# Twelve of 22 pairs of up tiles as seven block products for eight, and the inner tiles of one feed-forward in three parts

## The chip, the cores and the metric

The kernel runs on one core of one Trainium2 chip. The metric is the time of one execution on the device, in microseconds (us). A core has these engines: TensorE (PE) multiplies matrices, and its weight loads are shown apart as PEld; VectorE (DVE) and ScalarE (ACT) work on elements; GpSimd (POOL) does a few small operations; SyncE (SP) issues the DMA transfers. Each has its own queue of instructions and works it off in order; semaphores tie them together. Matmul results go to eight banks of 128 x 512 float32 (names b_...).

## The reference: what is computed

The reference is a float32 network for 256 latent tokens and 256 context tokens of width 1024. A first block (gated linear attention and a squared-ReLU feed-forward) is followed by two layers whose norms and residual sums are modulated by a conditioning vector: layer 0 with neighbourhood attention over latents and context, layer 1 with grouped-query attention. The change is in the feed-forward of layer 0, which runs over latents (h) and context (hc) with the same weights:

```python
def swiglu_ffn(h, w_in, w_out):
    a, g = jnp.split(h @ w_in, 2, axis=-1)
    return (jax.nn.silu(a) * g) @ w_out

h  = h  + g2_l * swiglu_ffn(ada_norm(h,  norm_ffn[i], sh2_l, sc2_l), ffn_w_in[i], ffn_w_out[i])
hc = hc + g2_c * swiglu_ffn(ada_norm(hc, norm_ffn[i], sh2_c, sc2_c), ffn_w_in[i], ffn_w_out[i])
```

`w_in` is 1024 x 5632, `w_out` 2816 x 1024. The modulation vectors (shifts, scales, gates g2_l, g2_c and the same for layer 1) are products of the conditioning vectors with a 1024 x 6144 matrix for each layer.

## The kernel before

**Products.** Every float32 product is made of three matmuls in a reduced format: each operand x is split into h (x rounded, an ACT copy) and l = x - h (a DVE subtract), and `mm3` issues h*h, l*h and h*l (lines 193, 194, 195). So a block of 128 x 128 weights by n token columns costs three matmuls.

**Weights.** All weights pass as a list of units (`UNITS`), each a tile of 128 x 1024. `w_load` sends a unit by SP into one of five "raw" buffers (512 KB), `w_split` makes its h on ACT (L178) and its l on DVE (L179) in two of the "w" buffers, and `wnext` hands it to the matmuls and runs the loads and splits some units ahead.

**The feed-forward of layer 0.** The 2816 inner features are 22 tiles of 128. For each, a pair of units (one of `a`, one of the gate `g`, each 1024 x 128) is multiplied with the transposed, normalised tokens `fT` (all 512 columns): 2 x 8 x 3 = 48 matmuls of 512 columns (`ffn_up`). The first two pairs run in two halves of 256 columns (`ffn_up_first`), while the latents are still transposed. Behind a pair, `ffn_act` makes Silu on ACT (L1111), the product with the gate on DVE (L1112) and the split of the result (ACT L1118, DVE L1119). The 22 tiles go in two parts of 11. After each part `ffn_down0` multiplies them with the down units: one bank for each of the token tiles 0 to 3 (0, 1 latents; 2, 3 context), half of the 1024 output columns (`hf`) at a time, and `gated` multiplies the banks with the modulation's gate and adds them to the residual (DVE L1080, L1081). In part 0 all four token tiles run together. In part 1 the context tiles run first, both halves, so that their normalisation (`normed`, L219) can run while the latents run; within the latents' last half, after some inner tiles, the context's transposes for layer 1 are issued (`to_T`, PE L232, then DVE and ACT conversions L248 to L251).

**The modulation.** The rest of the modulation vectors is computed on DVE beside all this: `ada_run(adaC, n)` takes n steps; a step loads a 128 x 1024 tile of the conditioning matrix by SP into one of two "ada" buffers and reduces it against the conditioning vector (L324, a multiply with a sum along the row), for some of the steps twice, for latents and context (double steps). Before, each up pair takes two steps and each down unit one.

**Order.** The code names the work in the order in which it is written, but a tile scheduler orders the instructions on each engine by its own estimate. What runs when on an engine is therefore seen in the compiled order, of which some rows are shown with the change.

## Time and profile before

| | us |
|---|---|
| runs shown: median of 3 (lowest to highest) | 1257.70 (1257.22 to 1257.75) |
| profiled execution, its own time | 1256.72 |
| its span in the trace | 1254.9 |
| PE busy | 1244.0 |
| DVE busy | 919.9 |
| ACT busy | 688.2 |
| the changed stage in the trace (first up pair to the end of the down product) | about 562 to 944 |

The profiled execution is 1.0 us below the median of the runs. The stage's up pairs of part 0 run to about 694, the down product of part 0 to about 755, the up pairs of part 1 to about 866, and the rest is the down product of part 1. In the rows below, "x" is a count, a name in front of "<-" is what is written, and the name behind "<-" in a row of waits is what was waited for. A row of a timeline begins with its start in us from the start of the span and its duration.

### The profile page before, as it was taken

What the parts mean: (1) busy time and instruction counts of PE and PEld (TensorE: products, weight loads), DVE (VectorE), ACT (ScalarE), POOL (GpSimd) and SP (SyncE); (2) the same over time, 40 slices, a digit from 0 to 9 for tenths busy, and PEclk for the clock granted to TensorE, in tenths of its full rate; (3) what the DMA queues carried; (4) which work ended last, traced back from release to release, by engine and by line L of the source; (5) the groups of instructions that cost most, each with busy time, mean ns of one, the idle gap of its engine ahead of it and who ended that gap; (6) DMA issues with size and microseconds to landing.
All of it is one profiled execution on the core that took longest, in us unless ns stands there. A gap on an engine that the chain in (4) does not pass through costs nothing.

```text
span 1254.9 us, 18667 instructions
## 1 busy us (share of the span) xinstructions
PE 1244.0 (99%) x6872; PEld 1043.2 (83%) x6872; DVE 919.9 (73%) x1638; ACT 688.2 (55%) x1344; POOL 78.7 (6%) x137
## 2 busy tenths in 40 slices
PE   9999999999999999999999999999999999999997
PEld 8888889898888777789888888887888777999997
DVE  6959888697989887777877767633667988655555
ACT  8575655666549888655232222323456897544443
POOL 1010000030100000001000000000003220000000
PEclk9999999999999999999999999999999999999999
DMA  8647687787673333463656877633662324656650
GB/s 304 189 151 237 192 289 268 271 277 246 198 249 111 105 110 118 160 197 118 213 177 206 259 266 249 205 100 102 197 204 76 113 84 131 219 187 185 186 185 34
DMA packets 68507, 231.22 MB, mean 184 GB/s; under 512 B 8048, under 2 KB 8736, under 8 KB 68416
## 3 DMA queue, kind: packets, MB, share of 16 engines
q1 hardware_dynamic: 68128, 229.68, 57.0%
q8 instruction: 54, 0.88, 0.3%
q10 hardware_dynamic: 288, 0.35, 0.1%
q14 instruction: 37, 0.30, 0.1%
HBM read 228.93 MB, written 1.07 MB: 183 GB/s over the span
## 4 chain that ended last, share of the span: by engine, by line
PE 95%; ACT 2%; DVE 1%; issue 1%; DMA 0%; POOL 0%; SPq 0%; POOLq 0%; ACTq 0%
PE b L193 28%; PE b L194 28%; PE b L195 28%; PE b L1000 2%; PE b L1469 1%; PE b L981 1%; PE b L232 1%; PE b L1455 1%; PE b L562 1%; PE b L962 1%; PE b L963 1%; PE b L951 1%; PE b L1436 1%; DVE wl L179 0%; DMA t<-in_xt_dram 0%
## 5 line engine op out<-in xcount | busy, mean ns | idle before, releaser
L178 ACT CAST wh<-raw 128x1024 fp32r<-128x1024 f32 (+1 forms) x308 | 320.7, 1045 | 392.8 <-PE b L194 292.4
L179 DVE TENSOR_TENSOR wl<-raw,wh 128x1024 fp32r<-128x1024 f32 (+1 forms) x308 | 372.5, 1216 | 154.9 <-ACT wh L178 151.9
L193 PE MATMUL b<-t,wh 128*128 128x256 f32 (+1 forms) x1120 | 365.7, 327 | 0.0
L194 PE MATMUL b<-t,wl 128*128 128x256 f32 (+1 forms) x1120 | 365.6, 327 | 0.0
L195 PE MATMUL b<-t,wh 128*128 128x256 f32 (+1 forms) x1120 | 365.3, 327 | 0.0
L193 PE MATMUL b<-wh,t 128*128 128x512 f32 (+1 forms) x748 | 299.2, 402 | 1.2 <-ACT t L250 0.6
L194 PE MATMUL b<-wh,t 128*128 128x512 f32 (+1 forms) x748 | 294.8, 394 | 0.0
L195 PE MATMUL b<-wl,t 128*128 128x512 f32 (+1 forms) x748 | 294.7, 394 | 0.0
L193 PEld LDWEIGHTS b<-t,wh 128*128 128x128 f32 x1120 | 210.7, 188 | 22.2
L194 PEld LDWEIGHTS b<-t,wl 128*128 128x128 f32 x1120 | 210.8, 188 | 21.9
L195 PEld LDWEIGHTS b<-t,wh 128*128 128x128 f32 x1120 | 210.5, 188 | 20.4 <-DVE t L251 0.2
L195 PEld LDWEIGHTS b<-wl,t 128*128 128x128 f32 x748 | 140.4, 188 | 34.2
L193 PEld LDWEIGHTS b<-wh,t 128*128 128x128 f32 x748 | 140.4, 188 | 32.2 <-ACT t L250 1.0
L194 PEld LDWEIGHTS b<-wh,t 128*128 128x128 f32 x748 | 140.8, 188 | 30.1 <-DVE t L251 0.5
L324 DVE CUSTOM_DVE_ANT_0 a<-a,crow 128x1024 f32<-128x1024 f32 x96 | 117.6, 1233 | 28.8 <-DMA a<-in_ada_dram 28.3
L324 DVE CUSTOM_DVE_ANT_0 t<-a,crow 128x1024 bf16<-128x1024 f32 x64 | 78.5, 1237 | 7.3 <-DMA a<-in_ada_dram 7.1
L1112 DVE TENSOR_TENSOR t<-b,t 128x512 f32<-128x512 f32 (+1 forms) x42 | 23.7, 564 | 59.4 <-PE b L195 52.2
L205 POOL TENSOR_TENSOR c<-c,mhalf 128x1 f32<-128x1 f32 x21 | 14.2, 676 | 539.0 <-DVE c L204 538.9
L339 POOL TENSOR_TENSOR mod<-mod,bcol 128x8 f32<-128x8 f32 x20 | 13.4, 671 | 475.1 <-DVE mod L324 472.7
L1118 ACT CAST t<-t 128x512 fp32r<-128x512 f32 (+1 forms) x42 | 21.7, 516 | 28.6 <-DVE t L1112 28.6
L212 ACT ACTIVATE t<-t 128x512 f32<-128x512 f32 x40 | 24.8, 624 | 10.8 <-DVE t L1081 6.4
L1445 ACT ACTIVATE t<-b,c,c 128x512 f32<-128x512 f32 x32 | 26.0, 812 | 3.5 <-POOL c L1443 3.5
(244 smaller groups left out, 1212.6 us busy)
## 6 DMA issues: line engine op xcount, KB each, us to landing
raw<-in_wst_dram SPq DMA_DIRECT2D x310, 512.0 KB, 4.4
a<-in_ada_dram SPq DMA_DIRECT2D x96, 512.0 KB, 4.4
t<-in_rpb_dram SPq DMA_DIRECT2D x16, 256.0 KB, 4.5
t<-row SPq DMA_DIRECT2D x12, 256.0 KB, 5.1
t<-in_ctx_dram SPq DMA_DIRECT2D x8, 256.0 KB, 5.6
t<-in_xt_dram SPq DMA_DIRECT2D x4, 256.0 KB, 5.8
t<-in_x_dram SPq DMA_DIRECT2D x4, 256.0 KB, 6.5
crow<-in_cvec_dram SPq DMA_DIRECT2D x2, 512.0 KB
```

Source lines behind the costliest of these rows:

```text
L178: A.copy(out=h[:, :n], in_=raw[:, :n])
L179: V.tensor_tensor(out=l[:, :n], in0=raw[:, :n], in1=h[:, :n], op=ALU.subtract)
L193: T.matmul(o, lhsT=lh, rhs=rh, start=first, stop=False)
L194: T.matmul(o, lhsT=ll, rhs=rh, start=False, stop=False)
L195: T.matmul(o, lhsT=lh, rhs=rl, start=False, stop=last)
L205: G.tensor_tensor(out=ms[:, 3:4], in0=ms[:, 2:3], in1=mhalf[:, 0:1], op=ALU.pow)
L212: A.activation(out=junk[hf], in_=halves[hf], func=AF.Square, scale=1.0 / 32.0, accum_out=ms[:, hf:hf + 1])
L324: V.tensor_tensor_reduce(out=raw if ci == n_c - 1 else t2([D], BF16), in0=raw, in1=crow[ci], scale=1.0, scalar=0.0, op0=ALU.mult, op1=ALU.add,
L1000: T.matmul(po[e * 64:(e + 1) * 64, cols_], lhsT=v, rhs=probs[(head, "l" if lat_q else "c")][:, c, :], start=(c == 0), stop=(c == n_c - 1))
L1112: V.tensor_tensor(out=a, in0=pg_[:, :n], in1=a, op=ALU.mult)
L1118: A.copy(out=h, in_=a)
L1445: A.activation(out=pl, in_=sl, func=AF.Exp, scale=r, bias=mx[:, 1:2], accum_out=mx[:, 2:3])
```

## The change

The 22 inner tiles go in three parts, 0 to 7, 8 to 15, 16 to 21 (`PARTS`), with a down product after each; there are 28 down units of full size instead of 36 of which six are half units. The tokens stand in two sets of 256 columns, `fL` (latents) and `fC` (context), so the ordinary pairs make 96 matmuls of 256 columns instead of 48 of 512.

From pair 10 on (`F_SEVEN`), a pair is computed in Strassen's manner. The pair's weights are a 2 x 2 matrix of blocks (a or g, by upper or lower half of the 1024 inputs), the tokens one too (half of the inputs, by latents or context). The ordinary product takes eight block products, the scheme seven, each of 4 x 3 matmuls of 256 columns: 84 a pair (`ffn_up7`). For it, sums of the weight blocks are made and split for each pair (`pair_sums`: DVE L1202, L1203, L1206, L1209; three full splits, ACT L1196 and DVE L1197, and a half one, L1211 and L1212), in three raw buffers and seven w buffers, and sums of the token blocks once (`token_sums`, in the second half of the first down product). Behind the products, DVE adds them up (L1238, L1248 to L1256, of 256 columns, L1260 of 512), between copies and Silus on ACT (L1235, L1241, L1242, L1247, L1255, L1259). Bank `r` takes four products one on top of the other, with ACT copies of it in between; `r23` takes two, `r4` one. The sums of a pair are issued while the pair before it is multiplied.

The modulation steps: two in each of the pairs 0 to 9, none in the later pairs, two in a down unit with four token tiles, one in the others. The context's transposes come after four of the last part's six inner tiles, with two inner tiles behind them. `load_gates` runs in every part.

The diff, cut to its core:

```diff
-HALF = NFT // 2
+PARTS = ((0, 8), (8, 16), (16, 22))
+F_SEVEN = 10
...
+    def seven(u):
+        return u[1] == "ffn_in0" and u[2] % FH >= P * F_SEVEN
     def wnext(kind):
         i = wpos[2]
         assert UNITS[i][:len(kind)] == kind, (UNITS[i], kind)
         wpos[2] += 1
         w_load(max(i + 1, wpos[1]) + 4)
         w_split(i + 1)
-        while wpos[1] < len(UNITS) and wpos[1] - wpos[2] + 1 < cap[0]:
+        while wpos[1] < len(UNITS) and wpos[1] - wpos[2] + 1 < cap[0] and not seven(UNITS[wpos[1]]):
             w_load(wpos[1] + 4)
             w_split(wpos[1] + 1)
...
+    fL, fC = new_T(), new_T()
+    fX = [t2([2, S]) for _ in range(KD)]
     o_half(1, 2, hc, 1)
     xn = [normed(t) for t in hc]
     o_half(0, 0, lat, 0)
-    o_half(1, 0, lat, 0, lambda: to_T(xn, fT, S, mod(0, 1, 4), mod(0, 1, 3)))
+    o_half(1, 0, lat, 0, lambda: to_T(xn, fC, 0, mod(0, 1, 4), mod(0, 1, 3), [z[:, 1, :] for z in fX]))
...
+    def ffn_up(L, src, n, conv=iter(())):
         ps_ = []
         for _ in range(2):
             u = wnext(("f", f"ffn_in{L}"))
             o = bank()
-            for k in range(KD):
-                mm_f(o[:, :n], u, src, k, 0, n, k == 0, k == KD - 1)
+            for t, X in enumerate(src):
+                for k in range(KD):
+                    mm_f(o[:, t * S:(t + 1) * S], u, X, k, 0, S, k == 0, k == KD - 1)
+            run(conv, 2)
...
+    def token_sums(j):
+        lo, hi, q = fX[j], fX[j + KD // 2], t2([2, S])
+        V.tensor_tensor(out=q[:, 1, :], in0=hi[:, 1, :], in1=lo[:, 1, :], op=ALU.subtract)
+        V.scalar_tensor_tensor(out=q[:, 0, :], in0=q[:, 1, :], scalar=-1.0, in1=lo[:, 0, :], op0=ALU.mult,
+                               op1=ALU.subtract)
+        V.tensor_tensor(out=lo[:, 1, :], in0=lo[:, 0, :], in1=lo[:, 1, :], op=ALU.subtract)
+        V.scalar_tensor_tensor(out=lo[:, 0, :], in0=q[:, 0, :], scalar=-1.0, in1=hi[:, 0, :], op0=ALU.mult,
+                               op1=ALU.subtract)
+        for z, names in ((q, (2, 1)), (lo, (4, 3))):
+            h, l = t2([2, S], F32R), t2([2, S], F32R)
+            A.copy(out=h, in_=z)
+            V.tensor_tensor(out=l, in0=z, in1=h, op=ALU.subtract)
+            for i, name in enumerate(names):
+                sT[(name, j)] = (h[:, i, :], l[:, i, :])
+    def pair_sums(f, got):
+        i = wpos[1]
+        assert UNITS[i] == ("f", "ffn_in0", P * f)
+        w_load(i + 4)
+        x, y = raws.pop(i), raws.pop(i + 1)
+        z = sb.tile([P, 1024], F32, tag="raw", bufs=5, name=nm("raw"))
+        wpos[1] += 2
+        a, b = slice(0, 512), slice(512, 1024)
+        def parts(r):
+            h = sb.tile([P, 1024], F32R, tag="w", bufs=NW, name=nm("wh"))
+            l = sb.tile([P, 1024], F32R, tag="w", bufs=NW, name=nm("wl"))
+            A.copy(out=h, in_=r)
+            V.tensor_tensor(out=l, in0=r, in1=h, op=ALU.subtract)
+            got.append((h, l))
+        parts(x)
+        yield
+        V.tensor_tensor(out=z[:, a], in0=x[:, a], in1=y[:, a], op=ALU.add)
+        V.tensor_tensor(out=z[:, b], in0=z[:, a], in1=y[:, b], op=ALU.add)
+        parts(z)
+        yield
+        V.tensor_tensor(out=y[:, a], in0=y[:, a], in1=y[:, b], op=ALU.add)
+        parts(y)
+        yield
+        V.tensor_tensor(out=x[:, a], in0=z[:, b], in1=x[:, b], op=ALU.add)
+        hl = sb.tile([P, 1024], F32R, tag="w", bufs=NW, name=nm("w"))
+        A.copy(out=hl[:, a], in_=x[:, a])
+        V.tensor_tensor(out=hl[:, b], in0=x[:, a], in1=hl[:, a], op=ALU.subtract)
+        got.append((hl[:, a], hl[:, b]))
+        yield
+    def splits(n):
+        for _ in range(n):
+            w_split(wpos[1] + 1)
+            yield
+    def ffn_up7(got, conv):
+        wpos[2] += 2
+        r, r23, r4 = bank(), bank(), bank()
+        c1, c2 = t2([2, S]), t2([2, S])
+        H = KD // 2
+        def prod(o, n, c, X, first=True):
+            h, l = got[n]
+            for j in range(H):
+                k = slice(c + j * P, c + (j + 1) * P)
+                mm3(o, h[:, k], l[:, k], *X(j), first and j == 0, j == H - 1, not first)
+        run(conv, 2)
+        prod(r[:, 0:S], 0, 0, lambda j: fL[j])
+        A.copy(out=c1[:, 0, :], in_=r[:, 0:S])
+        prod(r23[:, 0:S], 0, 512, lambda j: fL[H + j])
+        got[0] = None
+        V.tensor_tensor(out=c1[:, 0, :], in0=r23[:, 0:S], in1=c1[:, 0, :], op=ALU.add)
+        run(conv)
+        prod(r[:, 0:S], 1, 512, lambda j: sT[(2, j)], False)
+        A.copy(out=c1[:, 1, :], in_=r[:, 0:S])
+        A.activation(out=c1[:, 0, :], in_=c1[:, 0, :], func=AF.Silu)
+        prod(r23[:, S:N2], 2, 512, lambda j: sT[(4, j)])
+        run(conv)
+        prod(r[:, 0:S], 1, 0, lambda j: sT[(1, j)], False)
+        got[1] = None
+        A.copy(out=c2[:, 0, :], in_=r[:, 0:S])
+        V.tensor_tensor(out=c2[:, 1, :], in0=c1[:, 1, :], in1=c2[:, 0, :], op=ALU.subtract)
+        V.tensor_tensor(out=c2[:, 0, :], in0=r23[:, S:N2], in1=c2[:, 0, :], op=ALU.add)
+        V.tensor_tensor(out=c2[:, 0, :], in0=c2[:, 0, :], in1=c1[:, 0, :], op=ALU.mult)
+        prod(r4[:, 0:S], 3, 0, lambda j: fC[H + j])
+        V.tensor_tensor(out=c2[:, 1, :], in0=r4[:, 0:S], in1=c2[:, 1, :], op=ALU.add)
+        prod(r[:, 0:S], 2, 0, lambda j: sT[(3, j)], False)
+        V.tensor_tensor(out=c2[:, 1, :], in0=r[:, 0:S], in1=c2[:, 1, :], op=ALU.add)
+        A.activation(out=c2[:, 1, :], in_=c2[:, 1, :], func=AF.Silu)
+        V.tensor_tensor(out=c2[:, 1, :], in0=r[:, 0:S], in1=c2[:, 1, :], op=ALU.mult)
+        a = c2.rearrange("p t s -> p (t s)")
+        h, l = t2([N2], F32R), t2([N2], F32R)
+        A.activation(out=h, in_=a, func=AF.Copy, scale=-1.0)
+        V.scalar_tensor_tensor(out=l, in0=a, scalar=-1.0, in1=h, op0=ALU.mult, op1=ALU.subtract)
+        return h, l
...
+    def ffn_down0(hf, uu, tiles, between=None, conv=None):
         ac = {t: bank() for t in tiles}
-        for f2 in range(0, HALF, 2):
+        for f2 in range(0, len(uu), 2):
             u = wnext(("h", "ffn_out0"))
-            for j in range(min(2, HALF - f2)):
+            for j in range(2):
                 f = f2 + j
                 for t in tiles:
-                    mm_h(ac[t], u, j, uu[f], t, f == 0, f == HALF - 1)
-            ada_run(adaC)
-            if f2 == 4 and between is not None:
+                    mm_h(ac[t], u, j, uu[f], t, f == 0, f == len(uu) - 1)
+            ada_run(adaC, 2 if len(tiles) == 4 else 1)
+            if hf == 1 and len(sT) < 16:
+                token_sums(f2 // 2)
+            if conv is not None and f2 >= len(uu) - 4:
+                run(conv, 2)
+            if f2 == 2 and between is not None:
                 between()
...
+    for lo, hi in PARTS:
         uu = []
+        for f in range(lo, hi):
+            nxt = []
+            if f + 1 < hi:
+                conv = pair_sums(f + 1, nxt) if f + 1 >= F_SEVEN else iter(())
             else:
+                conv = splits(2) if f >= F_SEVEN else iter(())
+            if f < 2:
+                uu += ffn_up_first() if f == 0 else []
+            elif f < F_SEVEN:
+                uu.append(ffn_up(0, (fL, fC), N2, conv))
+            else:
+                uu.append(ffn_up7(got, conv))
+            got = nxt
+            if f < F_SEVEN:
+                ada_run(adaC, 2)
+        load_gates(0, 5)
+        if hi < NFT:
+            ffn_down0(0, uu, (2, 3, 0, 1))
+            got = []
+            ffn_down0(1, uu, (2, 3, 0, 1), None, pair_sums(hi, got) if hi >= F_SEVEN else None)
         else:
             for hf in range(2):
                 ffn_down0(hf, uu, (2, 3))
```

Three places in the compiled order. First DVE around an ordinary pair of part 1, before. L179 is a weight split, L324 a reduce of the modulation (with a short row that reads its sum), L1112 and L1119 what follows the pair:

```order
L179 TENSOR_TENSOR wl_7977<-raw_7852,wh_7976 128x1024
L324 ISA a_8273,mod_8195<-a_8273,crow_87 128x1024
L324 ISA mod_8195 128x1
L324 ISA a_8351,mod_8195<-a_8351,crow_87 128x1024
L324 ISA mod_8195 128x1
L1112 TENSOR_TENSOR t_7883<-b_7858,t_7883 128x512
L179 TENSOR_TENSOR wl_8008<-raw_7899,wh_8007 128x1024
L1119 TENSOR_TENSOR t_7887<-t_7883,t_7886 128x512
```

and DVE after the change, from the last reduce ahead of pair 11's weight sums to the end of these (L329 is the reduce's line now, L1238 the first sum behind the products of pair 10):

```order
L329 ISA a_7873,mod_7736<-a_7873,crow_87 128x1024
L329 ISA mod_7736 128x1
L1197 TENSOR_TENSOR wl_7886<-raw_7672,wh_7885 128x1024
L1202 TENSOR_TENSOR raw_7884<-raw_7672,raw_7742 128x512
L1238 TENSOR_TENSOR t_7882<-b_7880,t_7882 128x256
L1203 TENSOR_TENSOR raw_7884<-raw_7884,raw_7742 128x512
L1206 TENSOR_TENSOR raw_7742<-raw_7742 128x512
L1209 TENSOR_TENSOR raw_7672<-raw_7884,raw_7672 128x512
L1197 TENSOR_TENSOR wl_7892<-raw_7884,wh_7891 128x1024
L1197 TENSOR_TENSOR wl_7923<-raw_7742,wh_7922 128x1024
L1212 TENSOR_TENSOR w_7953<-raw_7672,w_7953 128x512
```

The two weight splits and two rows of a pair have become the sums and splits of the next pair and the rows behind the products of this one; reduces still stand in front. The second place is PE in pair 10, the first of the new kind, where the second product (into b_7880) ends and the third (into b_7881, which is `r4`) begins:

```order
L198 MATMUL b_7880<-t_5759,wh_7794 128x256
L199 MATMUL b_7880<-t_5759,wl_7795 128x256
L200 MATMUL b_7880<-t_5759,wh_7794 128x256
L198 MATMUL b_7881<-t_5764,w_7863 128x256
L199 MATMUL b_7881<-t_5764,w_7863 128x256
L200 MATMUL b_7881<-t_5764,w_7863 128x256
```

In the code the product into `r4` is the sixth of the pair; here it is the third, and it reads w_7863, the half tile. The third place is DVE where w_7863 is made, at the end of pair 10's sums, among the rows behind the ordinary pairs 8 and 9 (L1118 and L1125, the lines of L1112 and L1119 now):

```order
L1118 TENSOR_TENSOR t_7727<-b_7678,t_7727 128x512
L1197 TENSOR_TENSOR wl_7801<-raw_7793,wh_7800 128x1024
L1125 TENSOR_TENSOR t_7731<-t_7727,t_7730 128x512
L1206 TENSOR_TENSOR raw_7617<-raw_7617 128x512
L1209 TENSOR_TENSOR raw_7556<-raw_7793,raw_7556 128x512
L1118 TENSOR_TENSOR t_7866<-b_7808,t_7866 128x512
L1197 TENSOR_TENSOR wl_7859<-raw_7617,wh_7858 128x1024
L1212 TENSOR_TENSOR w_7863<-raw_7556,w_7863 128x512
```

w_7863 is the last of the pair's sums on DVE, behind the product with the gate of pair 9 (L1118, from b_7808).

More of the change, by code (lines that the diff above doesn't have):

```diff
@@ L164, in w_split @@
             raw = raws.pop(i)
[L165 removed]
+            n = 1024
             h = sb.tile([P, 1024], F32R, tag="w", bufs=NW, name=nm("wh"))
@@ L190, in wnext, with mm3 @@
         return convs.pop(i)
[L192 to L195 removed]
+    def mm3(o, lh, ll, rh, rl, first, last, onto=False):
+        T.matmul(o, lhsT=lh, rhs=rh, start=first, stop=False, skip_group_check=onto)
+        T.matmul(o, lhsT=ll, rhs=rh, start=False, stop=False, skip_group_check=onto)
+        T.matmul(o, lhsT=lh, rhs=rl, start=False, stop=last, skip_group_check=onto)
     def inv_root(o, ms, n, eps=EPS):
@@ L1147, in ffn_up_first @@
         return z
-    def ffn_down0(hf, uu, tiles, between=None):
+    sT = {}
+    def token_sums(j):
[12 more added lines that the diff above has]
+                sT[(name, j)] = (h[:, i, :], l[:, i, :])
```

45 lines of the change are left out of this document (14 added, 31 removed).

## The prediction

> **What bounds the kernel now.** I read the page first: the busy times, the clock row and the chain that ended last.
>
> ```profile
> PE 1244.0 (99%) x6872; PEld 1043.2 (83%) x6872; DVE 919.9 (73%) x1638; ACT 688.2 (55%) x1344; POOL 78.7 (6%) x137
> ...
> PEclk9999999999999999999999999999999999999999
> ...
> PE 95%; ACT 2%; DVE 1%; issue 1%; DMA 0%; POOL 0%; SPq 0%; POOLq 0%; ACTq 0%
> ```
>
> TensorE (PE) works 99% of the span at the full granted clock, and the chain runs through it for 95%. Then the waits of PE, to see whether anything in the changed stage holds it, and the windows of that stage: the up pairs of part 0, the down product of part 0, the up pairs of part 1, the down product of its context tiles.
>
> ```profile
> PE b L121 <- POOL mhalf L137: 1.3, 1, 1.3
> PE b L193 <- ACT t L250: 0.6, 1, 0.6
> ...
> 592.00:694.00 102.00, 102.00 (x438) 81.96 (x437) 78.27 (x116) 28.63 (x38) 2.64 (x4) 1.00 0.65 206
> 694.00:755.00 61.00, 61.00 (x263) 49.06 (x262) 44.58 (x67) 12.70 (x13) 1.52 (x3) 1.00 0.77 254
> 755.00:866.00 111.00, 111.00 (x476) 89.15 (x475) 57.45 (x77) 31.61 (x41) 3.35 (x3) 1.00 0.53 171
> 866.00:905.00 39.00, 39.00 (x169) 31.31 (x168) 20.93 (x25) 16.00 (x23) 0.31 (x1) 1.00 0.58 174
> ```
>
> In a window the third figure is PE's busy time and the fifth that of VectorE (DVE). PE has no gap anywhere in the stage, so every matmul removed there is time saved; but DVE is at 78.27 of 102 us in the first up pairs and 44.58 of 61 in the first down product. What the change gives to PE it takes from that margin, so everything below is a balance of PE against DVE.
>
> **Part A, the matmuls.** The distance of starts of back-to-back matmuls, from the timeline of PE, first and last row of each run:
>
> ```profile
> 690.12 0.40 PE L193 MATMUL b<-wh,t 128*128 128x512 f32 x1
> ...
> 711.12 0.40 PE L193 MATMUL b<-wh,t 128*128 128x512 f32 x1
> ...
> 1100.00 0.28 PE L193 MATMUL b<-t,wh 128*128 128x256 f32 x1
> ...
> 1104.10 0.28 PE L195 MATMUL b<-t,wh 128*128 128x256 f32 x1
> ```
>
> 90 matmuls of 512 columns in 21.00 us are 0.2333 each; 35 of 256 in 4.10 are 0.1171. An ordinary pair is 48 x 0.2333 = 11.20 us, a pair of seven products 7 x 4 x 3 = 84 x 0.1171 = 9.84: 1.36 less, 12 times, 16.3 us. The 8 ordinary pairs f = 2 to 9 become 96 matmuls of 256 columns, 11.24 instead of 11.20: +0.3. The down products only change their grouping. A = **-16.0 us** of PE work; the program's count of PE instructions grows by 816 = 12 x 36 + 8 x 48, as this has it.
>
> **What DVE pays for a row.** Durations overlap, so I cost by distance of starts:
>
> ```profile
> 687.93 1.22 DVE L324 CUSTOM_DVE_ANT_0 t<-a,crow 128x1024 bf16<-128x1024 f32 x1
> ...
> 691.36 1.22 DVE L179 TENSOR_TENSOR wl<-raw,wh 128x1024 fp32r<-128x1024 f32 x1
> ...
> 717.33 1.28 DVE L1080 TENSOR_TENSOR t<-b,t 128x512 f32<-128x512 f32 x2
> 718.53 1.28 DVE L1081 TENSOR_TENSOR t<-t,t 128x512 f32<-128x512 f32 x2
> ...
> 572.99 1.42 DVE L251 TENSOR_TENSOR t<-t,t 128x256 fp32r<-128x256 f32 x4
> ```
>
> Three rows of 1024 columns lie between 687.93 and 691.36: 1.143 each. Two of 512 take 1.20: 0.60 each. Four of 256 end after 1.42, the last lasting 0.42: 0.333 each. A pair of seven products costs DVE 3 x 1.143 + 5 x 0.60 for the weight sums and their splits, and 7 x 0.333 + 0.60 behind the products: 6.43 + 2.93 = 9.36 us, against 9.84 of PE. An ordinary pair needs 2 x 1.143 + 2 x 0.60 = 3.5 against 11.20. So the balance holds in a pair alone, with 0.48 us to spare, and fails for every modulation reduce (L324, 1.143) put into it. The rows of DVE shown with the change have this: where it had four rows a pair, and reduces to fill, it now has the pair's whole arithmetic ahead of PE, and two reduces still stand just ahead of pair 11's sums.
>
> **Part B, the seam before the first seven products.** As the rows of PE and DVE shown with the change have it, the scheduler lets PE take the product with w_7863 (into b_7881) third in pair 10, while DVE makes w_7863 last of the pair's sums (L1212), behind the rows of pairs 8 and 9. From the end of pair 7 to that row the order has on DVE 39 rows of 1024 (30 reduces, 9 splits), 32 of 512 and 16 of 256: 44.6 + 19.2 + 5.3 = 69.1 us. PE has 192 matmuls of 512 (both halves of the down product) and 192 + 24 of 256: 44.8 + 25.3 = 70.1. DVE begins behind PE by what the last pair's Silu, product and split take:
>
> ```profile
> 684.79 0.69 DVE L1112 TENSOR_TENSOR t<-b,t 128x512 f32<-128x512 f32 x1 [2.92 <-PE b L195]
> ...
> 686.17 0.69 DVE L1119 TENSOR_TENSOR t<-t,t 128x512 fp32r<-128x512 f32 x1
> 686.78 1.22 DVE L324 CUSTOM_DVE_ANT_0 t<-a,crow 128x1024 bf16<-128x1024 f32 x1
> ```
>
> Its next free row is at 686.78, 2.1 us after PE's end just ahead of 684.79. So with no idle time PE would wait 69.1 + 2.1 - 70.1 = 1.1. But DVE does idle, on the modulation tiles:
>
> ```profile
> DVE a L324 <- DMA a<-in_ada_dram: 28.3, 19, 4.0
> ...
> 706.16 1.23 DVE L324 CUSTOM_DVE_ANT_0 a<-a,crow 128x1024 f32<-128x1024 f32 x1 [1.84 <-DMA a<-in_ada_dram]
> 707.63 1.22 DVE L324 CUSTOM_DVE_ANT_0 a<-a,crow 128x1024 f32<-128x1024 f32 x1 [0.23 <-DMA a<-in_ada_dram]
> 711.84 1.23 DVE L324 CUSTOM_DVE_ANT_0 a<-a,crow 128x1024 f32<-128x1024 f32 x1 [1.84 <-DMA a<-in_ada_dram]
> 713.84 1.23 DVE L324 CUSTOM_DVE_ANT_0 a<-a,crow 128x1024 f32<-128x1024 f32 x1 [0.77 <-DMA a<-in_ada_dram]
> ```
>
> Two buffers in turn: one read until 707.39 is read anew at 711.84, one read until 708.85 at 713.84: 4.7 us from release to use. The change takes two steps of two reduces in each unit of the first down half. A turn of both buffers is 4.7 + 2 x 1.143 = 7.0 us, four units 28.0, in which DVE has 16 reduces and 4 splits, 22.9 us: 5.1 us idle, and behind each waiting reduce stand the weight splits and the rows that free banks. For these late rows I add one gated round held, 8 x 0.60 = 4.8 (the other pair of banks must be read before PE can go on); ends none and two rounds. **B = 1.1 + 5.1 + 4.8 = +11.0**, from 1.1 (loads land in time) to 15.8.
>
> Apart from the sum: in the rows PE never stands over 1.3 us and its clock never drops, so no row here prices a long stall. The Trainium skill, "TensorE: Matmul & The Clock Gate", section "HAM oscillation — how this bites in real kernels", lets the clock fall after idle gaps over some 3.4 us, with a cold time of half speed; by it one such stall in B would add an estimated 1.7 us. I leave it out.
>
> **Part C, pairs 11 to 15.** Between the sums of pairs 10 and 15 the order has on DVE 21 rows of 1024 (15 splits, 6 reduces), 30 of 512, 28 of 256: 24.0 + 18.0 + 9.3 = 51.3, against 5 x 9.84 = 49.2 of PE: +2.1. A busy DVE also loses its own waits: it stands for ScalarE's (ACT) Silu of 256 columns between two of its rows, and for a bank's copy, each about
>
> ```profile
> L1111 ACT ACTIVATE t<-b 128x256 f32<-128x256 f32 x20 | 7.6, 379 | 1.6 <-PE b L195 1.6
> L251 DVE TENSOR_TENSOR t<-t,t 128x256 fp32r<-128x256 f32 x40 | 15.5, 421 | 3.5 <-ACT t L250 3.1
> L178 ACT CAST wh<-raw 128x1024 fp32r<-128x1024 f32 x302 | 317.0, 1054 | 382.0 <-PE b L194 285.7 <-issue 74.3 <-DMA a<-in_ada_dram 9.1
> ```
>
> 0.42 + 0.38 - 0.333 = 0.47, twice a pair: 0.94. Ends: none, and one product (12 x 0.1171 = 1.4) a pair. **C = 2.1 + 5 x 0.94 = +6.8**, 2.1 to 9.1. ACT's copy of a bank between two products into it has 1.4 us of cover: it takes 0.38, behind one cast 1.05 + 0.38 = 1.43, so nothing.
>
> **Parts D and E.** The second group, pairs 16 to 21, has no reduces: 9.36 under 9.84, so 0, up to 2 if it starts late. At the end of the stage, these rows say how late the context comes to its transposes:
>
> ```profile
> 900.32 0.69 DVE L1080 TENSOR_TENSOR t<-b,t 128x512 f32<-128x512 f32 x1 [1.42 <-PE b L195]
> 908.01 0.88 DVE L219 TENSOR_SCALAR t<-t,c 128x512 f32<-128x512 f32 x2 [0.66 <-POOL c L205]
> ...
> 924.62 1.69 PE L232 MATMUL b<-cm,t 128*128 128x128 f32 x14
> ```
>
> From 900.3 to 908.9 runs the normalisation; before, 11 + 6 inner tiles of the latents lay over it (6 matmuls, 1.40 us each: 23.8), now 6 + 4 (14.0), and behind the transposes 2 (2.8) instead of 5 (7.0). 14.0 covers 8.6, but the latents' four gated rows now fall into it: **E = 4 x 0.60 = +2.4**, from 0 to the 4.2 us lost behind the transposes. The DMAs are not the limit: 8 units fewer are loaded.
>
> **The sum.** -16.0 + 11.0 + 6.8 + 0 + 2.4 = **+4.2 us**. On the profiled execution's 1256.7 that is 1260.9; the median of the runs shown, 1257.7, is 1.0 above it: **1262**.
>
> **Rivals.** *DVE keeps up*: loads land in time, no row is held, waits hide behind other rows. Then B = 1.1, C = 2.1, E = 0: -12.8, 1245; with the late loads alone (B = 6.2) -7.7, 1250. For it: 78.27 of 102 was without any loss, and DVE's rows before the seam are 1 us fewer than PE's. Against: two buffers, and 19 waits for them already. This is the faster side; it decides whether the 5.1 us of idle DVE time reach PE. 0.20. *Half of the losses*: B 8.6, C 4.4, E 1.2: -1.8, no change. 0.13. *ACT blocks the banks*: two casts ahead of one copy in each pair, 2 x 1.05 + 0.38 - 1.4 = 1.1, 12 times 13: slower, 1275. Against: ACT is busy 55%. 0.08. *DVE pays its durations*: rows 1.23, 0.69 and 0.42, 3 x 1.23 + 5 x 0.69 + 7 x 0.42 + 0.69 = 10.8 a pair over 9.84: another 12 us for the twelve pairs, and 7 more in the seam, 1281. The rows above speak against it (1.143 and 0.60 where the duration is 1.22 and 0.69): 0.04. In its sentence: the Trainium skill, "VectorE: DVE Perf Modes", section "The DRAIN you can't avoid", says the next operation begins when the pipe is empty, unless it is not held; the trace shows the second.
>
> **How the numbers follow.** The sum's case 0.52, the four rivals 0.20, 0.13, 0.08, 0.04, the rest 0.03. Its own range is 1257 to 1268; the ends of all terms reach 1245 and 1273. Leaving out a tenth on each side: 1249 to 1271. About 0.2% (2.5 us) is what can be told from no change. Faster: the first rival, 0.20. Same: the second and the low edge of the sum, 0.16. Slower: the rest, 0.64.
>
> **What would show it.** PE busy about 16 us lower, and PE's waits about 20: one or two stalls at L198 of together 5 us or more ahead of the third product of the first seven (released by L1197 or L1212 of DVE), DVE busy over 95% from there through pair 15, reduces waiting for DMA in the first down half; about 1 us a pair in the first group, almost none in the second; a wait of 1 to 3 us at the last transposes. Wrong, if the waits of PE in the stage stay under 12 us, or if they are released by ACT's copies.

## The result: 1272.7 us against 1257.7, and the profile after

The changed kernel takes 1272.68 us (median of 4 runs, 1272.24 to 1274.30), the kernel before 1257.72 (1257.22 to 1258.05): ratio 1.0122, 95% interval 1.0104 to 1.0139, 15.0 us slower. The direction was forecast, the size was not: +4.2 us stood there, and 1272.7 lies just above the range (1249 to 1271). The span of the profiled execution is 1271.0 us against 1254.9.

From the page of the changed kernel, busy times, chain and the loads of the gate rows (12 before, with 5.1 us to landing), and from the view of PE's waits the longest rows:

```profile
PE 1241.7 (98%) x7688; PEld 1077.7 (85%) x7688; DVE 1003.5 (79%) x1814; ACT 718.9 (57%) x1416; POOL 79.2 (6%) x137
...
PE 81%; DVE 9%; DMA 4%; ACT 3%; issue 2%; POOL 0%; SPq 0%; POOLq 0%; ACTq 0%; DVEq 0%
...
t<-row SPq DMA_DIRECT2D x20, 256.0 KB, 6.2
```

```profile
PE b L198 <- ACT w L1211: 6.8, 2, 5.6
PE b L237 <- DVE t L253: 1.9, 1, 1.9
PE b L198 <- ACT t L1235: 1.9, 2, 1.2
PE b L237 <- DVE t L224: 1.9, 2, 0.9
PE b L198 <- DVE t L1085: 1.4, 1, 1.4
```

Before, the chain lay on PE for 95% and no wait of PE was over 1.3 us. Now 9% of the chain lies on DVE and 4% on the loads of modulation tiles. PE's busy time fell by only 2.3 us, although its matmuls became 16 us shorter: a slower clock took part of that. In four stretches of the stage (start and end, length, then busy time of PE, PEld, DVE, ACT and POOL, then the granted clock):

```profile
697.00:745.00 48.00, 40.20 (x312) 39.12 (x311) 46.45 (x83) 15.26 (x24) 0.58 (x1) 0.93 0.53 170
745.00:800.00 55.00, 51.16 (x381) 48.18 (x380) 52.88 (x90) 29.17 (x49) 0.59 (x1) 0.97 0.57 193
800.00:900.00 100.00, 99.87 (x659) 90.26 (x659) 85.04 (x134) 39.06 (x62) 1.17 (x2) 1.00 0.51 165
900.00:965.00 65.00, 59.68 (x290) 47.74 (x290) 47.54 (x83) 35.06 (x68) 2.55 (x4) 0.97 0.46 154
```

and the same stretches of the kernel before, in the same columns:

```profile
697.00:745.00 48.00, 48.00 (x208) 38.60 (x207) 33.44 (x51) 9.04 (x9) 1.52 (x3) 1.00 0.78 256
745.00:800.00 55.00, 55.00 (x237) 44.21 (x235) 41.38 (x61) 14.51 (x19) 2.23 (x2) 1.00 0.78 256
800.00:900.00 100.00, 100.00 (x430) 80.28 (x429) 42.04 (x47) 31.80 (x41) 1.12 (x1) 1.00 0.43 130
900.00:965.00 65.00, 65.00 (x306) 52.68 (x305) 49.12 (x95) 37.70 (x82) 8.48 (x12) 1.00 0.53 162
```

In the changed kernel, 697 to 745 holds the end of the first down product, pairs 8 and 9 and the first seven-product pair; 745 to 800 the rest of the first group and the passage to the second down product; 800 to 900 that product and the second group; 900 to 965 the end of the stage. To count waits and slow clock together I use one more figure, worked out from PE's timeline: **lost PE time**, the sum over all matmuls of the distance to the next start, less the full-speed distance (0.2333 us for 512 columns, 0.1171 for 256, 0.105 for the transposes). In these four stretches it was 0.0, 0.2, 0.3 and 0.2 us before, and is 11.4, 7.9, 2.3 and 8.9 now.

**The first seam.** DVE from the first half of the down product to the half tile of pair 10 (rows left out between):

```profile
664.30 1.23 DVE L329 CUSTOM_DVE_ANT_0 t<-a,crow 128x1024 bf16<-128x1024 f32 x1 [2.85 <-DMA a<-in_ada_dram]
...
675.25 1.23 DVE L329 CUSTOM_DVE_ANT_0 t<-a,crow 128x1024 bf16<-128x1024 f32 x1 [1.07 <-DMA a<-in_ada_dram]
...
721.10 1.28 DVE L1085 TENSOR_TENSOR t<-b,t 128x512 f32<-128x512 f32 x2
...
731.17 0.68 DVE L1212 TENSOR_TENSOR w<-raw,w 128x512 fp32r<-128x512 f32 x1
```

and PE at the same place:

```profile
721.93 0.36 PE L198 MATMUL b<-t,wh 128*128 128x256 f32 x1 [1.44 <-DVE t L1085]
730.57 0.58 PE L198 MATMUL b<-t,w 128*128 128x256 f32 x1 [5.56 <-ACT w L1211]
731.91 0.58 PE L199 MATMUL b<-t,w 128*128 128x256 f32 x1 [0.76 <-DVE w L1212]
732.29 0.41 PE L200 MATMUL b<-t,w 128*128 128x256 f32 x1
...
735.70 0.41 PE L198 MATMUL b<-t,w 128*128 128x256 f32 x1
```

DVE idles on modulation loads in the first half (2.85, 0.20, 1.07 and 0.69 us, 4.8 in all), then runs almost without a gap to 731. The gated rows at 721.10 free banks 1.44 us late, the half tile comes 5.56 us late, as foretold at that product. Behind the long wait the matmuls go at half speed: the 17 starts from 732.29 to 735.70 are 0.213 us apart, where 0.117 is full speed. A window of it (the granted clock is the 0.68):

```profile
731.00:739.00 8.00, 7.19 (x41) 6.78 (x41) 7.62 (x13) 2.48 (x7) 0.00 (x0) 0.68 0.75 252
```

**The end of the stage.** DVE between the context's banks and the conversions of its transposes, then PE:

```profile
929.68 1.29 DVE L1085 TENSOR_TENSOR t<-b,t 128x512 f32<-128x512 f32 x2 [2.16 <-DMA t<-row]
...
938.42 0.88 DVE L224 TENSOR_SCALAR t<-t,c 128x512 f32<-128x512 f32 x2 [0.44 <-POOL c L210]
...
939.82 1.21 DVE L180 TENSOR_TENSOR wl<-raw,wh 128x1024 fp32r<-128x1024 f32 x1
...
941.56 2.35 DVE L180 TENSOR_TENSOR wl<-raw,wh 128x1024 fp32r<-128x1024 f32 x2
943.83 0.54 DVE L253 TENSOR_SCALAR t<-b,mod,mod 128x256 f32<-128x256 f32 x1
```

```profile
937.06 0.74 PE L237 MATMUL b<-cm,t 128*128 128x128 f32 x5 [0.93 <-DVE t L224]
938.96 0.77 PE L237 MATMUL b<-cm,t 128*128 128x128 f32 x5 [0.93 <-DVE t L224]
944.42 0.44 PE L237 MATMUL b<-cm,t 128*128 128x128 f32 x2 [1.89 <-DVE t L253]
946.77 0.47 PE L198 MATMUL b<-wh,t 128*128 128x512 f32 x1 [1.01 <-DVE t L253]
```

PE waits for the normalisation of each of the two token tiles (L224), then for banks that the conversions (L253) free late, because three weight splits (L180) and the latents' rows stand in front of them on DVE. The residual rows of the context began with a wait of 2.16 us for the gate rows, which the change loads anew for each part.

### The profile page after: what moved, and what is told of

The parts are those of the page before. It is cut to its first block, busy times and chain, and to the rows that moved or that the text cites. A ratio compares the mean times of both kernels' runs of the same rounds, so it can differ in the third digit from the quotient of the medians.

```text
span 1271.0 us, 20578 instructions
## 1 busy us (share of the span) xinstructions
PE 1241.7 (98%) x7688; PEld 1077.7 (85%) x7688; DVE 1003.5 (79%) x1814; ACT 718.9 (57%) x1416; POOL 79.2 (6%) x137
## 3 DMA queue, kind: packets, MB, share of 16 engines
HBM read 226.83 MB, written 1.07 MB: 179 GB/s over the span
## 4 chain that ended last, share of the span: by engine, by line
PE 81%; DVE 9%; DMA 4%; ACT 3%; issue 2%; POOL 0%; SPq 0%; POOLq 0%; ACTq 0%; DVEq 0%
PE b L198 24%; PE b L199 23%; PE b L200 23%; DMA a<-in_ada_dram 3%; PE b L1005 2%; DVE a L329 2%; PE b L1598 1%; DVE wl L1197 1%; PE b L986 1%; DVE wl L180 1%; PE b L1584 1%; DVE t L329 1%; PE b L237 1%; PE b L567 1%; DVE t L1085 1%
## 5 line engine op out<-in xcount | busy, mean ns | idle before, releaser
L179 ACT CAST wh<-raw 128x1024 fp32r<-128x1024 f32 x276 | 289.2, 1053 | 271.7 <-PE b L199 224.2
L180 DVE TENSOR_TENSOR wl<-raw,wh 128x1024 fp32r<-128x1024 f32 x276 | 336.3, 1227 | 129.4 <-ACT wh L179 127.2
L198 PE MATMUL b<-t,wh 128*128 128x256 f32 (+1 forms) x1344 | 394.3, 294 | 3.6 <-ACT t L1235 1.9
L199 PE MATMUL b<-t,wl 128*128 128x256 f32 (+1 forms) x1344 | 392.5, 292 | 0.0
L200 PE MATMUL b<-t,wh 128*128 128x256 f32 (+1 forms) x1344 | 391.8, 292 | 0.0
L198 PEld LDWEIGHTS b<-t,wh 128*128 128x128 f32 x1344 | 253.9, 189 | 15.2 <-ACT t L1247 2.6
L199 PEld LDWEIGHTS b<-t,wl 128*128 128x128 f32 x1344 | 254.3, 189 | 7.6
L200 PEld LDWEIGHTS b<-t,wh 128*128 128x128 f32 x1344 | 253.9, 189 | 5.8 <-DVE t L256 0.2
L329 DVE CUSTOM_DVE_ANT_0 a<-a,crow 128x1024 f32<-128x1024 f32 x96 | 117.0, 1225 | 8.0 <-DMA a<-in_ada_dram 7.6
L329 DVE CUSTOM_DVE_ANT_0 t<-a,crow 128x1024 bf16<-128x1024 f32 x64 | 78.8, 1237 | 11.7 <-DMA a<-in_ada_dram 11.4
L1196 ACT CAST wh<-raw 128x1024 fp32r<-128x1024 f32 x36 | 37.5, 1048 | 35.9 <-DVE raw L1203 10.8
L1197 DVE TENSOR_TENSOR wl<-raw,wh 128x1024 fp32r<-128x1024 f32 x36 | 43.6, 1219 | 4.2 <-ACT wh L1196 2.2
L1118 DVE TENSOR_TENSOR t<-b,t 128x256 f32<-128x256 f32 (+1 forms) x30 | 15.4, 513 | 28.9 <-PE b L200 25.2
L217 ACT ACTIVATE t<-t 128x512 f32<-128x512 f32 x40 | 24.8, 623 | 14.8 <-DVE t L1086 10.4
```

Of the source, the lines that this page charges most:

```text
L179: A.copy(out=h[:, :n], in_=raw[:, :n])
L180: V.tensor_tensor(out=l[:, :n], in0=raw[:, :n], in1=h[:, :n], op=ALU.subtract)
L198: T.matmul(o, lhsT=lh, rhs=rh, start=first, stop=False, skip_group_check=onto)
L199: T.matmul(o, lhsT=ll, rhs=rh, start=False, stop=False, skip_group_check=onto)
L200: T.matmul(o, lhsT=lh, rhs=rl, start=False, stop=last, skip_group_check=onto)
L217: A.activation(out=junk[hf], in_=halves[hf], func=AF.Square, scale=1.0 / 32.0, accum_out=ms[:, hf:hf + 1])
```

## The experiments

Each time stands beside runs of the kernel before on the same chip (medians 1257.0 to 1257.7). "Lost" is the lost PE time of the profiled execution in the four stretches 697 to 745, 745 to 800, 800 to 900 and 900 to 965 us; in kernels with other parts these hold somewhat different work.

| kernel | median us | ratio to before (95%) | lost in the four stretches |
|---|---|---|---|
| before | 1257.7 | | 0.0, 0.2, 0.3, 0.2 |
| the change | 1272.7 | 1.0122 (1.0104 to 1.0139) | 11.4, 7.9, 2.3, 8.9 |
| 1 parts only, no seven products | 1262.1 | 1.0034 (1.0021 to 1.0046) | 0.6, 0.6, 0.9, 1.7 |
| 2 modulation steps spread | 1263.8 | 1.0047 (1.0032 to 1.0062) | 3.7, 5.6, 4.7, 9.1 |
| 3 parts of 8, 6, 8 | 1270.1 | 1.0104 (1.0089 to 1.0119) | 13.2, 4.2, 11.3, 2.6 |
| 4 half tile early | 1269.2 | 1.0097 (1.0079 to 1.0114) | 11.2, 4.7, 3.3, 8.6 |
| 5 reduces cut short | 1263.5 | 1.0062 (1.0042 to 1.0082) | 7.0, 3.4, 2.3, 8.4 |
| 6 edits 2 and 3, gate rows early | 1257.6 | 1.0007 (0.9998 to 1.0016) | 3.4, 3.6, 8.3, 0.8 |
| 7 gate rows early | 1269.2 (one run) | | 11.6, 7.7, 3.6, 6.0 |
| 8 splits' lookahead late | 1267.9 (one run) | | 10.6, 7.9, 2.6, 6.6 |
| 9 as 6, half tile early | 1257.1 | 0.9995 (0.9985 to 1.0005) | 4.5, 1.9, 9.2, 0.3 |
| 10 as 6, six seven-product pairs | 1256.3 | 0.9992 (0.9982 to 1.0001) | 0.6, 0.3, 5.1, 0.2 |
| 11 edits 7 and 8 | 1272.4 (one run) | | 12.8, 7.7, 3.5, 5.9 |
| 12 as 10, steps earlier | 1254.3 | 0.9974 (0.9965 to 0.9983) | 0.6, 0.3, 3.3, 0.3 |

**1. The parts without the seven products.**

```diff
-F_SEVEN = 10
+F_SEVEN = 22
-            if hf == 1 and len(sT) < 16:
+            if hf == 1 and len(sT) < 16 and F_SEVEN < NFT:
```

> The three parts, the two token sets and the gate loads of the change, with all 22 pairs ordinary (no pair sums, no token sums, no seven products). Theory T: the loss at the end of the stage (about 8 us of lost PE time between 930 and 962 us after the change) comes from the short last part of six inner tiles, not from the seven products, so it stays here: before plus 8 for it, plus 0.8 for 20 pairs in 256 columns, plus 1 to 2 elsewhere: 1267 us, and no wait of PE in the up pairs. Rival R: DVE is late at the end only because of the rows behind the seven products: then this costs 1 to 3 us over before: 1260.

1262.1, nearer to R. The windows of 800 to 900 and of the end:

```profile
800.00:900.00 100.00, 100.00 (x706) 93.34 (x706) 38.31 (x44) 24.61 (x31) 0.00 (x0) 1.00 0.28 92
900.00:965.00 65.00, 64.05 (x309) 51.88 (x308) 47.81 (x84) 36.64 (x78) 5.85 (x8) 1.00 0.48 152
```

With the same short last part PE loses 1.7 us at the end, not 8.9. Ahead of it DVE is busy for 38 of 100 us, in the change for 85. So the short cover alone does not make the loss; run 3 shows the other side. The restructuring alone costs 4.4 us, for which my sum had 0.3 (0.8 if all 20 pairs are counted) and the 2.4 of the end.

**2. Modulation steps spread.** Nothing is left out.

```diff
-            ada_run(adaC, 2 if len(tiles) == 4 else 1)
+            ada_run(adaC, (1 if lo == 0 else 2) if len(tiles) == 4 else 2)
-            if f < F_SEVEN:
+            if f < 8:
                 ada_run(adaC, 2)
```

> The change with the modulation steps spread otherwise: two in each of pairs 0 to 7, one (not two) in a unit of the first down product, none in pairs 8 and 9, two in the units of the second and third down product. Nothing is left out. Theory T: the seam's stall (8.8 us of waits and about 2 of a slower clock) and the waits of pairs 11 to 15 (about 8 us) come from the reduces in front of the sums on DVE; with 14 reduces (16 us of DVE) out of the stretch the waits for L1211 and L1212 there fall under 1 us, those of the first group to about 2, and the time to about 1256. Rival R: the chain of copies, Silus and banks inside a seven-product pair makes the waits, and reduces only fill gaps: 1268 to 1272.

8.9 us faster than the change, half of what T said was to be had. The first seam falls from 11.4 to 3.7, which bears T out there; the first group only from 7.9 to 5.6, and the second now loses 4.7. The scheduler's order is one reason: the code has no step in the pairs of the groups, but the compiled order puts reduces between the sums again. Six of them (L329) stand from 845 to 900 us, where the change has none, and DVE is busy for 91.4 us from 800 to 900 instead of 85.0. The windows of 697 to 745 and 800 to 900:

```profile
697.00:745.00 48.00, 45.89 (x381) 45.09 (x380) 48.00 (x83) 20.25 (x32) 0.64 (x2) 1.00 0.46 149
...
800.00:900.00 100.00, 97.84 (x638) 87.82 (x637) 91.42 (x144) 41.70 (x64) 0.79 (x2) 1.00 0.58 187
```

**3. Parts of 8, 6 and 8.**

```diff
-PARTS = ((0, 8), (8, 16), (16, 22))
+PARTS = ((0, 8), (8, 14), (14, 22))
```

> The change with parts of 8, 6 and 8 inner tiles instead of 8, 8 and 6: four seven-product pairs in the second part, eight in the third. Theory T: two more inner tiles under the context's normalisation and behind its transposes take the loss at the end of the stage from 8 us to 3 or less; seam and first group stay (one or two pairs fewer wait): 1266. Rival R: the end is late because DVE is late behind the seven products: unchanged there or worse, 1271 to 1274.

The end loses 2.6 instead of 8.9, as T said: the cover is enough with eight tiles. But the second group, now of eight pairs right behind the second down product, loses 11.3 instead of 2.3, and the median gains only 2.6 (the profiled execution, 1272.95, is the slowest of the four). So T was right about the end, but had not foreseen the second group: the time, 1270.1, is nearer to R's 1271 than to T's 1266. The loss moved.

**4. The half tile first.** `hl` (L1209, L1211, L1212) is made before the splits of the other two sums.

```diff
-        parts(z)
-        yield
-        V.tensor_tensor(out=y[:, a], in0=y[:, a], in1=y[:, b], op=ALU.add)
-        parts(y)
-        yield
         V.tensor_tensor(out=x[:, a], in0=z[:, b], in1=x[:, b], op=ALU.add)
         ...
+        parts(z)
+        yield
+        V.tensor_tensor(out=y[:, a], in0=y[:, a], in1=y[:, b], op=ALU.add)
+        parts(y)
```

> The change with the half tile of the pair's sums (the operand of the product that PE takes third) made ahead of the other two splits. Theory T: DVE's total decides, so the 5.6 us wait for the half tile gets shorter by what is moved behind it (one add and two splits, 2.9 us), and most of that returns as waits for the tiles moved behind: 1270 to 1273. Rival O: it is the order alone, PE stalls for a tile that is needlessly last: the wait falls under 3 us, the clock does not drop, and the same happens in each pair of the first group: 1263 to 1267.

The waits of PE between 697 and 800 us (L1206 and L1207 are the half tile's lines in this kernel):

```profile
PE b L198 <- ACT w L1206: 3.6, 2, 2.9
PE b L199 <- DVE wl L1197: 1.8, 2, 1.6
PE b L199 <- DVE w L1207: 1.5, 2, 0.8
```

In the seam T is right: the wait for the half tile is 2.9 us instead of 5.6, a wait of 1.6 for a full split comes instead, and the stretch loses 11.2 as before. In the first group the order did matter: 4.7 instead of 7.9. The total, 3.5 us less, lies just below T's 1270.

**5. Reduces cut short.** The reduces from the feed-forward's gate on read 64 of 1024 columns, so these modulation vectors are incomplete.

```diff
+                m = 64 if (L, v) not in ((0, 0), (0, 1), (0, 2), (0, 3), (0, 4)) else D
-                V.tensor_tensor_reduce(out=raw if ci == n_c - 1 else t2([D], BF16), in0=raw, in1=crow[ci], scale=1.0,
+                V.tensor_tensor_reduce(out=(raw if ci == n_c - 1 else t2([D], BF16))[:, :m], in0=raw[:, :m],
+                                       in1=crow[ci][:, :m], scale=1.0,
```

> The change with every reduce of the modulation from the feed-forward's gate on cut to its first 64 of 1024 columns (about 1.1 us of DVE less each; the loads stay; so these modulation vectors are left incomplete). Theory T: the reduces on DVE make the seam and most of the first group's waits: both together, 19 us of lost PE time after the change, fall under 5, the second group (2 us) and the end of the stage (8 us) stay, since no reduce lies in them: about 1258. Rival R: the chain of bank copies and Silus holds PE inside each pair: the first group keeps 5 us or more, as after the other spread of the steps: 1262 or more.

```profile
697.00:745.00 48.00, 44.41 (x352) 43.82 (x351) 37.86 (x89) 17.94 (x29) 0.52 (x2) 0.93 0.71 233
745.00:800.00 55.00, 53.54 (x391) 49.71 (x390) 42.19 (x90) 28.18 (x45) 0.40 (x2) 1.00 0.67 229
```

The two stretches lose 10.4 instead of 19.3: 8.9 of it goes, a little under half, where T had said that more than 14 would. R's sign for the first group, 5 us or more, did not come either (3.4), though the time lies in R's range. What is left need not be the chain inside a pair, for the loads of the modulation tiles stay in this run, and DVE stands for them for 6.0 us of the seam's 48. Two rows of DVE, then the two waits of PE in the seam:

```profile
720.99 0.23 DVE L330 CUSTOM_DVE_ANT_0 a<-a,crow 128x64 f32<-128x64 f32 x1 [2.10 <-DMA a<-in_ada_dram]
...
725.98 0.23 DVE L330 CUSTOM_DVE_ANT_0 a<-a,crow 128x64 f32<-128x64 f32 x1 [2.13 <-DMA a<-in_ada_dram]
```

```profile
723.93 0.39 PE L198 MATMUL b<-t,wh 128*128 128x256 f32 x1 [2.19 <-ACT t L1237]
727.69 0.58 PE L198 MATMUL b<-t,wh 128*128 128x256 f32 x1 [1.40 <-DVE t L1240]
```

The bank's copy (L1237) stands on ACT behind a row that waited for a DVE row (L1120, at 722.27) close behind the reduce of 720.99, and the product's sum (L1240) comes on DVE 1.2 us after the reduce of 725.98. The third wait, 1.46 us for a half tile at 754.06, follows two more loads, for which DVE stood 2.21 and 1.18 us until 747.06. So the modulation steps hold PE here by their loads as well as by their length; how much of the rest is the order in which sums and products are queued was not tested apart. The second group (2.3) and the end (8.4) stay, as T said. The time is 9.2 us below the change.

**6. Three edits together.** Those of 2 and 3, and the gate rows loaded two pairs ahead of their down product:

```diff
+            if lo and f == hi - 2:
+                load_gates(0, 5)
...
-        load_gates(0, 5)
+        if lo == 0:
+            load_gates(0, 5)
```

> Three edits together: the other spread of the modulation steps (one in a unit of the first down product, none in pairs 8 and 9, two in later units), parts of 8, 6 and 8 tiles, and the gate rows loaded two pairs ahead of their down product. If the gains add up (8.9 us of the spread, 6 at the end from the longer last part, 2 of the gate rows) and the longer last group loses 6: 1258 to 1262. Rival: what the last group of eight pairs loses is DVE's lateness from the reduces before it, and goes with the spread: 1252 to 1256, faster than the kernel before.

1257.6: just below the first case's 1258, and no difference from the kernel before that can be measured. The end is repaired (0.8), but the long last group keeps 8.3 us of loss. This does not refute the rival's mechanism: the compiled order put reduces into the group itself, ten from 840 to 900 us, so lateness from reduces did not go with the spread.

**7. Gate rows early**, the third edit of 6 alone, and **8. lookahead of splits late**:

```diff
-            cap[0] = 7
             ffn_down0(1, uu, (0, 1), lambda: to_T(xn, bT2, S, mod(1, 1, 1), mod(1, 1, 0)))
+            cap[0] = 7
```

> The change with the gate rows of the second and third part loaded two pairs ahead of the down product. Theory G: the new load of the rows (DVE waited 2.2 us for it ahead of the context's residual sums) is on the path to the transposes: the lost time at the end of the stage falls from 8 to about 6 us: 1270. Rival: DVE's own queue behind it (weight splits and the latents' rows in front of the transposes' conversions) takes the gain: no change, 1272 to 1273.

> The change with the lookahead of weight splits raised to seven only behind the feed-forward's last half. Theory: at the end of the stage three or four weight splits (1.14 us each) stand on DVE between the normalisation and the conversions of the transposes, while PE waits for banks: without them the lost time there falls from 8 to 5 us: 1269. Rival: the splits only move, and the projection behind waits for them: no change.

In the profiles the end loses 2.9 us less with the first and 2.3 less with the second, which is near the 2 and 3 that the theories gave. The times, one run each, 1269.2 and 1267.9, agree in direction, but other stretches differ by a microsecond or so between these executions, so neither gain is shown by the time.

**9. As 6, with the half tile early.**

> The three edits together (spread of the steps, parts of 8, 6 and 8, gate rows early) and the half tile made ahead of the other splits. After the three edits PE still loses about 12 us between 700 and 880 us to the sums of the pairs. If the order of the sums holds PE, as it did by 3.5 us in the change itself, 1254; if DVE's total decides, 1257 to 1258.

1257.1, no change: the first group loses less (1.9), the second more (9.2), which speaks for DVE's total and not for the order alone. One profiled execution each does not settle it.

**10. Six seven-product pairs.** As 6, with `F_SEVEN = 16`.

> The three edits, with seven products only from pair 16 on: six pairs instead of twelve, all in the last part, none beside the modulation's later steps. It saves 6 x 1.36 = 8.2 us of matmuls instead of 16.3. Theory T: a seven-product pair leaves DVE 0.5 us of slack, so each one within reach of other DVE work loses what it saves; six fewer of them take 6 to 9 us of the 12 us of lost PE time away: 1255 to 1257, as fast as with twelve. Rival: the loss sits in each pair alike (chain of copies and Silus), about 1 us each, so six fewer lose 6 and save 8 less: 1259.

1256.3, T's case: the six pairs that are left out cost 8.2 us of matmuls more, and of the 16.1 us lost 9.9 go. What is left in the second group is one wait of 2.2 us for a bank's copy at the first seven-product pair, behind a reduce that waited 2.05 us for its load, and smaller ones.

**11. Both edits of 7 and 8.**

> The change with both edits at the end of the stage: gate rows two pairs early and the lookahead of splits raised late. Alone they took 2.9 and 2.3 of the 8.9 us that PE loses from 900 us on. If the loss there is DVE's queue between the context's banks and the conversions, they add up: 4 us left, 1267. Rival: each removes the same delay, 6 us left, 1269.

They don't add up: 5.9 us are lost from 900 on, as with the first alone. One wait took the place of several, and splits still stand in front of the conversions, whatever the lookahead (DVE, then PE):

```profile
941.66 2.35 DVE L180 TENSOR_TENSOR wl<-raw,wh 128x1024 fp32r<-128x1024 f32 x2
943.92 0.42 DVE L256 TENSOR_TENSOR t<-t,t 128x256 fp32r<-128x256 f32 x1
944.26 2.36 DVE L180 TENSOR_TENSOR wl<-raw,wh 128x1024 fp32r<-128x1024 f32 x2
```

```profile
947.55 0.47 PE L198 MATMUL b<-wh,t 128*128 128x512 f32 x1 [2.87 <-DVE t L253]
```

The time, 1272.4 in one run, shows no gain at all; 1.4 us more were lost in the seam and 1.2 in the second group. That the rival's number (6 us) came out does not settle which row made the delay.

**12. Six pairs, steps earlier.** As 10, with two steps in each of the pairs 0 to 13 and one in each unit of the first two down products.

```diff
-            ada_run(adaC, (1 if lo == 0 else 2) if len(tiles) == 4 else 2)
+            ada_run(adaC, (1 if lo == 0 else 1) if len(tiles) == 4 else 2)
-            if f < 8:
+            if f < 14:
                 ada_run(adaC, 2)
```

> Six seven-product pairs in the last part of eight (as in the run before with six), with the modulation's steps taken two in every ordinary pair 0 to 13, one in a unit of the first two down products: so they are done earlier and fewer stand before the first seven-product pair, where PE lost 2.3 us in one wait. If that wait was DVE's lateness from the reduces and their loads, it goes: 1253 to 1255, faster than the kernel before by 0.2%. Rival: the wait moves to the next sum, 1256 to 1257.

1254.3 us (median of 11 runs, 1253.0 to 1255.4): ratio 0.9974, interval 0.9965 to 0.9983, faster than both kernels. The wait of 2.2 us is gone, and PE has hardly a gap:

```profile
800.00:900.00 100.00, 99.45 (x761) 94.60 (x761) 81.50 (x126) 47.53 (x73) 1.12 (x1) 1.00 0.45 146
900.00:965.00 65.00, 65.00 (x307) 52.48 (x305) 51.59 (x101) 39.74 (x88) 9.39 (x12) 1.00 0.47 151
```

Of the 8.2 us that six pairs save, 3.1 arrive as a difference to the kernel before; the rest went to what the other edits cost and to the 3.3 us still lost from 800 to 900, in shares that no run separates.

## Why the prediction was right in its direction and wrong in its size

**Step A held.** Against the trace before, the trace after has 960 matmuls of 512 columns fewer and 1776 of 256 columns more; at the full-speed distances that is -16.0 us, as forecast.

**Step B had the right sum for a partly wrong reason.** It said +11.0; 11.4 were lost. DVE's idle time on loads was 4.8 (5.1 forecast), and the place and the waiting product were as foretold. But the round of gated rows that I added as held (4.8) shows as only 1.4 us of wait for L1085. The waits (1.44, 5.56 and 0.76 us in the rows above) came to 8.8, counted by the distances of starts; about 2.2 more were the slower clock behind the long one, which I had left out of the sum. That the total fits is therefore in part luck. The Trainium skill, "TensorE: Matmul & The Clock Gate", section "HAM oscillation — how this bites in real kernels", speaks of idle gaps over some 3.4 us; the trace agrees for the long wait, 5.56 us and then a granted clock of 0.68 from 731 to 739; the last section has a slower clock behind shorter waits.

**Step C was slightly low.** +6.8 forecast; the stretch from 745 to 800 us lost 7.9, the passage to the second down product included. Of this the reduces made more than the 2.1 I had from counting rows: without their length 3.4 is left (run 5), so 4.5 went with it.

**Step D was low:** 0 forecast, 2.3 lost, of which only 0.3 in a gap over 0.25 us; the rest is small delays between the products.

**Step E failed, and it makes the largest part of the miss.** It said +2.4, "14.0 covers 8.6", with ends of 0 and 4.2; 8.9 were lost. I had taken PE's cover from the code's order and DVE's chain from the trace before. The compiled order puts much of the context's down product between the last up pairs (in the trace from 893.7 us on), and DVE comes to the end after 85 busy us of 100. The latents' four gated rows, which were the whole price of E, do stand in front of the conversions; but so do four weight splits of 1.14 us each, between 934.49 and 943.83, and ahead of them the wait of 2.16 us for the gate rows, for which E had nothing. Runs 1 and 3 show the two sides: with ordinary pairs in front 1.7 is lost, with two more tiles of cover 2.6. Which row of DVE weighs most was not settled (runs 7, 8 and 11) and stays open. The 20 loads of gate rows for 12 stood in the code, and I costed them at nothing.

**A term was missing.** Outside the four stretches PE lost 2.3 us more than before in the profiled execution (14.0 against 12.65 before 560 us, 7.3 against 6.6 behind 965, and 0.2 between 560 and 697). In the twelve runs the first of these figures lies between 13.0 and 14.4, in kernels that are the same there as code; its cause stays open.

Against +4.2 the terms give, each less what the kernel before lost in the same stretch: E 6.3 more, the missing term 2.3, D 2.0, C 0.9, B 0.4: +16.1, and the spans differ by 16.1.

**Rivals.** That DVE keeps up was wrong, and what was said to decide did decide: behind its 4.8 us of idle time DVE runs almost without a gap to the half tile, and PE stands 5.56 us for it. No run takes that idle time away alone, so this is read from the trace; run 2, with fewer steps in the first down product, lost 3.7 us in the seam instead of 11.4. *ACT blocks the banks* did not come: PE waited for a bank's copy (L1235) twice, 1.9 us in all, and not in each pair. Row durations do not set DVE's pace: it was busy 46.5 of 48 us in the seam and ran its rows at the distances used. Of the signs named, PE's waits of about 20 us came (distances of starts over 0.25 us too long add up to 20.5 in the four stretches), but 6.4 of them lie at the end, where 1 to 3 had been foretold, and PE's busy time is not 16 us lower, since it counts matmuls at half clock and late ones as busy.

## What to carry to other kernels

Fewer matmuls are worth their time only where the engines that feed them have room left: here a seven-product pair saves 1.36 us of PE and raises DVE from 3.5 to 9.4 us in 9.8, so other DVE work near it turned into waits of PE. Six such pairs, with the modulation's steps moved ahead of them and eight tiles in the last part, made the kernel 0.26% faster; twelve, as in the change, made it 1.2% slower, and twelve with edits of the same kind (run 6) no faster or slower. Before costing the end of a stage, read the cover from the compiled order of both engines and count every transfer that the new loop repeats.

## What the runs showed of the hardware that was not expected

Behind one wait of 5.56 us the starts of matmuls of 256 columns were 0.213 instead of 0.117 us apart, for about 5.4 us. The clock also fell behind shorter waits: PE stood 1.21 us for the half tile until 782.9 and 0.56 us until 783.9, and then starts were again 0.213 apart until 787.2. The first two of the windows below show the clock at 0.96 and 0.59. But neither a single wait of 1.21 us (until 760.3, for a bank's copy) nor two of 0.93 us at the end (until 937.1 and 939.0) was followed by it: in the windows around them, the third and fourth, the clock is 1.00, and at the end it fell only behind three more waits, to 0.79 from 944 to 952. What decides between these cases was not measured.

```profile
782.00:784.00 2.00, 0.51 (x2) 0.32 (x2) 2.00 (x5) 1.98 (x5) 0.59 (x1) 0.96 0.83 256
784.00:788.00 4.00, 4.00 (x20) 3.81 (x21) 3.21 (x6) 1.46 (x4) 0.00 (x0) 0.59 0.93 304
...
757.00:764.00 7.00, 5.79 (x49) 5.58 (x49) 7.00 (x12) 5.16 (x9) 0.00 (x0) 1.00 0.34 105
...
936.00:944.00 8.00, 4.66 (x25) 3.30 (x24) 7.51 (x13) 3.83 (x4) 1.32 (x2) 1.00 0.43 132
```

So the price of a wait is not only its length: of the 28 us lost in the first two stretches and the last, some 5 to 6 were matmuls at half clock.
